# Layer 0 of a four-layer decoder trunk: one load for both gate matrices, three elementwise products on GpSimd, and a list scheduler that prices transfers

## The chip, the core and the metric

The kernel runs on one core of a Trainium2 chip. The metric is the device time of one launch in microseconds: 1310.87 us as the median of three runs (1310.73 to 1312.02). The engines are called as in the profile: PE is TensorE (PEld its weight loads), DVE is VectorE, ACT is ScalarE, POOL is GpSimd, SP is SyncE, which here only issues transfers.

## The reference, cut to what matters

One sequence of 256 tokens of width 1024 goes through four layers. Each layer has a token mixer, a SwiGLU network of hidden width 2816 and a gated embedding add, all between RMS norms. Layers 1 to 3 mix by attention. Layer 0, where the change lies, mixes by a gated linear recurrence:

```python
def rglru_block(h, w_in, conv_w, conv_b, gate_r_w, gate_r_b, gate_i_w, gate_i_b, a_param, w_out):
    u = h @ w_in
    y = jax.nn.gelu(u[..., :LRU_WIDTH], approximate=True)
    xb = u[..., LRU_WIDTH:]
    xp = jnp.pad(xb, ((0, 0), (CONV_WIDTH - 1, 0), (0, 0)))
    xc = conv_b
    for tap in range(CONV_WIDTH):
        xc = xc + xp[:, tap:tap + S] * conv_w[tap]
    xh = xc.reshape(B, S, LRU_BLOCKS, LRU_BLOCK_DIM)
    r = jax.nn.sigmoid(jnp.einsum('bsnd,nde->bsne', xh, gate_r_w).reshape(B, S, LRU_WIDTH) + gate_r_b)
    ig = jax.nn.sigmoid(jnp.einsum('bsnd,nde->bsne', xh, gate_i_w).reshape(B, S, LRU_WIDTH) + gate_i_b)
    log_a = -RGLRU_C * r.astype(jnp.float32) * jax.nn.softplus(-a_param.astype(jnp.float32))
    a = jnp.exp(log_a)
    mult = jnp.sqrt(-jnp.expm1(2.0 * log_a))
    b = mult * (ig * xc).astype(jnp.float32)
    _, hs = lax.associative_scan(_lin_rec_combine, (a, b), axis=1)
    return (hs.astype(h.dtype) * y) @ w_out
```

The two gate matrices are block diagonal: 16 blocks of 64 by 64 each.

## The kernel before

**How the products are made.** Every weight is read once from memory in chunks of 1 MB (a raw tile, `rawp_raw`, three buffers), and each half chunk is split into a high part (an ACT cast, `splitp_hi`) and a remainder (a DVE subtraction, `splitp_lo`), nine buffers of each. A product is then three matmuls: high by high, high by low, low by high. The activations are split in the same way (`ap_hThi`, `ap_hTlo`; in layer 0 `ap_A` and `ap_B`). The two halves of the sequence, 128 tokens each, follow each other through all layers, one some steps behind the other, so that PE has the matmuls of one half while the other half waits for a norm or a softmax.

**Layer 0.** `rglru_in` (line 657) normalizes x, turns it and multiplies it by `a_w_in` in four products of 512 columns each. The first two give the convolution's input, and for each of them `recurrence` (line 748) runs with tiles of 128 partitions by 4 x 256 elements. It runs in two halves: columns 0 to 511 of the recurrence from the first product, columns 512 to 1023 from the second; they are called the first and the second half below. A half goes like this. ACT starts `xc` from the product in PSUM, and DVE adds three taps to it for each of four column tiles (12 instructions). PE multiplies `xc` by the block-diagonal gate matrices `bd` (tiles `w_5` and `w_6`), ACT makes the sigmoids `la` (tile `w_2`) and `ig` (`w_3`) and scales `la`. DVE evaluates a polynomial of `la` in `e` (`w_4`) and subtracts one from `ex` (`w_7`, an exponential from ACT). It also compares `la` with a threshold in `msk` (`w_8`), and where the mask is set it replaces the polynomial by `ex` (line 783, `copy_predicated`). ACT takes the root, DVE multiplies `ig` by `xc` and by the root, and four scans give the state in the tile of `xc`. `gated` (line 795) multiplies it with the gelu of the third and fourth product, and `rglru_out` (line 1154) multiplies the result by `a_w_out`.

**The gate matrices.** Lines 659 to 665 clear `bd[0]` and `bd[1]` by a POOL memset each and load the 64 by 64 blocks straight into the diagonal by two transfers for each gate. A row of a block is 256 bytes, and so is a piece of these transfers.

**What sets the order.** The program is first recorded, not issued: each call becomes an entry with the entries that it must wait for. `price` (line 243) gives each a cost and `delay` (line 273) what a result takes to be seen on another engine. `pack` (line 286) is a list scheduler: going forward in time, each engine takes of the entries that are ready the one with the highest priority, and ACT holds back a function that needs another table (`SWITCH`). `schedule` (line 337) packs backward and forward ten times and keeps the order with the earliest end. Line 166 then issues everything, so that every instruction of the profile has line 166. The order on each engine is thus fixed when the kernel is built, and an engine takes its instructions strictly one after another. Transfers of weights are issued by SP, also in that order; an issue that has to wait for a free buffer holds up all issues behind it.

## Time and profile before

| | before |
|---|---|
| median of 3 runs | 1310.87 us (1310.73 to 1312.02) |
| the profiled execution | 1311.69 us, span 1309.9 us |
| PE busy | 1294.6 us, 99% |
| DVE busy | 943.4 us, 72% |
| ACT busy | 757.1 us, 58% |
| POOL busy | 36.2 us, 3% |
| granted PE clock | 0.998 |

The span is the time from the first to the last instruction on the core; the launch took 1.8 us more. A row of a timeline gives the start in us, the duration, the engine, the line and operation, the tiles written and read, and in brackets how long the engine had been idle and what ended that. Buffer numbers are left out of the tile names, so that `w_n` stands for many tiles. Busy times of matmuls overlap, since one starts before the last has left the array: of a row of equal matmuls the distance from start to start is the price.

### The profile page before, as it was taken

The numbers are of one execution on the slowest core, as the hardware profiler recorded it, in microseconds if no ns is written. First come the engines' busy times: TensorE is split into PE (matmuls) and PEld (weight loads), VectorE is DVE, ScalarE is ACT, GpSimd is POOL, SyncE is SP. The second block draws the span as 40 slices with busy tenths as digits, with TensorE's granted clock in tenths as the row PEclk, the third lists the DMA queues.
The fourth block names the chain that finished last, engine by engine and source line by source line (L and its number), as shares of the span: only waits on it lengthen the run. The fifth ranks groups of instructions, "written<-read, shape, count | busy, mean of one in ns | idle before, by whom it ended". The sixth has DMA issues, their size and how long they took to land.

```text
span 1309.9 us, 17008 instructions
## 1 busy us (share of the span) xinstructions
PE 1294.6 (99%) x6226; PEld 1051.8 (80%) x6226; DVE 943.4 (72%) x1598; ACT 757.1 (58%) x1308; POOL 36.2 (3%) x62
## 2 busy tenths in 40 slices
PE   8999999999999999999999999999999999999997
PEld 8978888887777888888777788888887788888886
DVE  7999666679765766667877676666788768666675
ACT  6975444456876644446666564444567666444453
POOL 1000000001000000000000000000000000000000
PEclk9999999999999999999999999999999999999999
DMA  9467666665444767767543476776655346667660
GB/s 311 154 210 208 209 209 203 208 201 191 131 159 136 221 206 206 208 211 227 193 133 133 137 224 205 203 204 209 215 180 187 121 137 221 208 209 201 208 191 33
DMA packets 214692, 247.62 MB, mean 189 GB/s; under 512 B 56784, under 2 KB 173776, under 8 KB 214608
## 3 DMA queue, kind: packets, MB, share of 16 engines
q1 hardware_dynamic: 166736, 234.99, 55.3%
q10 hardware_dynamic: 47872, 11.55, 5.3%
q8 instruction: 49, 0.80, 0.2%
q14 instruction: 35, 0.29, 0.1%
HBM read 233.92 MB, written 1.05 MB: 179 GB/s over the span
## 4 chain that ended last, share of the span: by engine, by line
PE 92%; ACT 3%; DVE 2%; DMA 1%; issue 0%; SPq 0%; POOL 0%; POOLq 0%; DVEq 0%; ACTq 0%
PE psU_u_n L166 55%; PE psY_y_n L166 34%; PE psT_t_n L166 3%; DMA rawp_raw_n<-in_a_w_in_dram 1%; ACT w_n L166 1%; ACT splitp_hi_n L166 1%; DVE w_n L166 1%; ACT L166 1%; DVE splitp_lo_n L166 1%; DVE ap_t_n L166 0%; DVE y_n L166 0%; DVE cp_x_n L166 0%; SPq L166 0%; ACT y_n L166 0%; POOL tp_sm_n L166 0%
## 5 line engine op out<-in xcount | busy, mean ns | idle before, releaser
L166 DVE TENSOR_TENSOR splitp_lo_n<-rawp_raw_n,splitp_hi_n 128x1024 fp32r<-128x1024 f32 x420 | 512.0, 1224 | 202.0 <-ACT splitp_hi_n L166 201.4
L166 ACT CAST splitp_hi_n<-rawp_raw_n 128x1024 fp32r<-128x1024 f32 x420 | 438.4, 1049 | 288.6 <-PE psU_u_n L166 187.4
L166 PE MATMUL psU_u_n<-splitp_hi_n,ap_hThi_n 128*128 128x512 f32 x992 | 394.5, 399 | 0.0
L166 PE MATMUL psU_u_n<-splitp_lo_n,ap_hThi_n 128*128 128x512 f32 x992 | 391.9, 395 | 0.4 <-DVE splitp_lo_n L166 0.4
L166 PE MATMUL psU_u_n<-splitp_hi_n,ap_hTlo_n 128*128 128x512 f32 x992 | 389.8, 396 | 0.0
L166 PEld LDWEIGHTS psU_u_n<-splitp_hi_n,ap_hTlo_n 128*128 128x128 f32 x992 | 186.4, 188 | 43.9 <-issue 1.0
L166 PEld LDWEIGHTS psU_u_n<-splitp_hi_n,ap_hThi_n 128*128 128x128 f32 x992 | 186.7, 188 | 43.6 <-issue 1.3
L166 PEld LDWEIGHTS psU_u_n<-splitp_lo_n,ap_hThi_n 128*128 128x128 f32 x992 | 186.5, 188 | 42.8 <-issue 1.7
L166 PE MATMUL psY_y_n<-splitp_hi_n,y_n 128*128 128x512 f32 x352 | 136.1, 394 | 0.0
L166 PE MATMUL psY_y_n<-splitp_hi_n,w_n 128*128 128x512 f32 x352 | 133.7, 396 | 0.0
L166 ACT ACTIVATE w_n<-psU_u_n,tp_sm_n 128x256 f32<-128x256 f32 (+1 forms) x96 | 47.3, 493 | 123.8 <-PE psU_u_n L166 79.0
L166 PE MATMUL psY_y_n<-splitp_hi_n,ap_hThi_n 128*128 128x512 f32 x208 | 82.3, 399 | 2.5 <-DVE y_n L166 1.4
L166 DVE SCALAR_TENSOR_TENSOR w_n<-psU_u_n,tp_sm_n,w_n 128x256 f32<-128x256 f32 x88 | 42.5, 483 | 56.0 <-ACT w_n L166 55.5
L166 PE MATMUL psY_y_n<-splitp_lo_n,ap_hThi_n 128*128 128x512 f32 x208 | 82.4, 398 | 0.0
L166 PE MATMUL psY_y_n<-splitp_hi_n,ap_hTlo_n 128*128 128x512 f32 x208 | 81.5, 395 | 0.0
L166 PEld LDWEIGHTS psY_y_n<-splitp_hi_n,y_n 128*128 128x128 f32 x352 | 66.1, 188 | 15.5
L166 PEld LDWEIGHTS psY_y_n<-splitp_hi_n,w_n 128*128 128x128 f32 x352 | 66.0, 188 | 14.5
L166 PE MATMUL psY_y_n<-splitp_lo_n,w_n 128*128 128x512 f32 x176 | 70.0, 397 | 0.0
L166 PE MATMUL psY_y_n<-splitp_lo_n,y_n 128*128 128x512 f32 x176 | 69.5, 395 | 0.0
L166 POOL TENSOR_TENSOR tp_sm_n<-tp_sm_n,cp_half_neg_n 128x1 f32<-128x1 f32 (+1 forms) x44 | 32.6, 742 | 1138.1 <-DVE tp_sm_n L166 1132.7
L166 ACT ACTIVATE w_n<-w_n,tp_sm_n 128x128 f32<-128x128 f32 (+1 forms) x112 | 46.9, 448 | 14.5 <-DVE tp_sm_n L166 14.4
L166 PEld LDWEIGHTS psY_y_n<-splitp_hi_n,ap_hThi_n 128*128 128x128 f32 x208 | 39.1, 188 | 12.1 <-issue 2.5
(145 smaller groups left out, 1407.4 us busy)
## 6 DMA issues: line engine op xcount, KB each, us to landing
rawp_raw_n<-in_w_ffn_in_dram SPq DMA_DIRECT2D x176, 512.0 KB, 4.7
rawp_raw_n<-in_w_ffn_out_dram SPq DMA_DIRECT2D x40, 1024.0 KB, 5.0
rawp_raw_n<-in_w_ple_gate_dram SPq DMA_DIRECT2D x16, 1024.0 KB, 5.1
rawp_raw_n<-in_b_w_qkv_dram SPq DMA_DIRECT2D x16, 512.0 KB, 4.4
rawp_raw_n<-in_c_w_qkv_dram SPq DMA_DIRECT2D x16, 512.0 KB, 4.5
rawp_raw_n<-in_d_w_qkv_dram SPq DMA_DIRECT2D x16, 512.0 KB, 4.5
rawp_raw_n<-in_a_w_in_dram SPq DMA_DIRECT2D x6, 1024.0 KB, 9.9
rawp_raw_n<-in_w_ffn_out_dram SPq DMA_DIRECT2D x8, 512.0 KB, 4.7
```

The lines of the kernel that those rows point to most:

```text
L166: getattr(engine.real, op)(*[self.bind(v) for v in args], **{k: self.bind(v) for k, v in kw.items()})
```

## The change

**One load.** The host lays both gate matrices out as one array `gates` of 128 partitions by 2 x 8 x 64 elements. One transfer of 4096 bytes in each partition brings it into the tile that is later `ex` (`w_7`), and POOL copies the blocks into the diagonals, two copies for each gate (64 partitions each).

**Three products on POOL.** In each half of the recurrence the subtraction of one from `ex`, the comparison that makes `msk`, and the product of `ig` with `xc` go from DVE to POOL.

**Casts.** The four casts that make `Hhi`, the high part of layer 0's activations, go from DVE to ACT.

**The scheduler.** Transfers get a model of their own (`Wires`): bytes over a rate, one after another, and a weight is no longer ready 2000 ns after its issue but when the model says it has landed; a transfer holds SP for 470 ns. PE gets kinds of matmul (whole array, 64 rows, 64 columns) between which a change costs 55 ns and is put off. Matmuls of 512 columns are priced at 232 instead of 216 ns, a result of ACT or DVE is seen by PE after 145 instead of 230 ns, POOL's products get prices of their own, 24 rounds are made instead of 10, and in every second round an engine may wait for a more urgent entry. The other new names (`XX`, `XQK`, `XP`, `GBY` and so on) stand at values that leave the code as it was.

```diff
@@
-ROUNDS = 10
-SWITCH = 3000
+ROUNDS = 24
+PEKEEP = 1000
@@
+DMA_ISSUE, DMA_FIRST, DMA_RATE, DMA_TOLD = 470, 1400, 385, 250
+CHANGE = {"ACT": (1283, 3000), "PE": (55, PEKEEP)}
...
+class Wires:
+    def __init__(self):
+        self.busy = 0.0
+    def land(self, eng, op, t, size):
...
+        self.busy = max(self.busy, t + DMA_FIRST) + size / DMA_RATE
+        return self.busy + DMA_TOLD
@@ def price(eng, op, args, kw):
-            return 1.68 * w / (P / math.prod(kw["lhsT"].shape[1:])) + 2
-        return 0.417 * w + 3
+            return 1.70 * w / (P / math.prod(kw["lhsT"].shape[1:])) + 6
+        return 0.4427 * w + 5.5
...
     if eng == "POOL":
-        return 36 + 0.83 * wide if op == "memset" else 300 + 165 * wide
+        if op in ("tensor_copy", "tensor_scalar"):
+            return 150 + 1.2 * wide
+        if op == "tensor_tensor" and kw["op"] != ALU.pow:
+            return 150 + 2.2 * wide
+        return 36 + 0.83 * wide if op == "memset" else 400 + 165 * wide
...
+    if op == "tensor_tensor_scan":
+        return 2.09 * wide + 48
@@ def delay(a, b, op=None):
-    return 230 if b == "PE" else 160 if b == "POOL" else 135
+    return 145 if b == "PE" else 160 if b == "POOL" else 135
@@ def pack(prog, forth, edges, need, prio, span=None):
+        if span is not None and e in ("PE", "DVE", "ACT"):
+            late = [r for r, j in f if r < t + cost[i] / 2 and prio[j] < p and t + cost[i] > span + prio[j] + 5
+                    and r + cost[j] <= span + p]
+            if late:
+                free[e] = min(late)
+                continue
...
+        lands = None
+        if forth and prog.size[i] is not None:
+            lands = wires.land(e, prog.ops[i][1], t, prog.size[i])
+            free[e] = t + (XBAR_ISSUE if prog.ops[i][1] == "dma_start_transpose" else DMA_ISSUE)
+            end = max(end, lands)
+        else:
+            free[e] = t + hold + cost[i]
@@ def rglru_in():
+        blocks = rg([P, 2, KT, 64], F32, "ex")
+        nc.sync.dma_start(out=blocks, in_=a["gates"])
         bd = []
-        for g, name in enumerate(("a_gate_r_w", "a_gate_i_w")):
+        for g in range(2):
             t = rg([P, KT, P], F32, "gw")
             G.memset(t, 0.0)
-            wv = a[name][0].rearrange("(n two) d e -> two d n e", two=2)
             for e in range(2):
-                nc.sync.dma_start(out=t[e * 64:(e + 1) * 64, :, e * 64:(e + 1) * 64], in_=wv[e])
+                h_ = slice(e * 64, (e + 1) * 64)
+                G.tensor_copy(out=t[h_, :, h_], in_=blocks[h_, g])
             bd.append(t)
@@
-                V.tensor_copy(out=Hhi[:, k, tk], in_=H[h][:, k, :])
+                A.copy(out=Hhi[:, k, tk], in_=H[h][:, k, :])
@@ def recurrence(f0, U):
-            V.tensor_scalar(out=ex, in0=ex, scalar1=-1.0, scalar2=None, op0=ALU.add)
-            V.tensor_scalar(out=msk, in0=la, scalar1=-E_RANGE / 2, scalar2=None, op0=ALU.is_lt)
+            G.tensor_scalar(out=ex, in0=ex, scalar1=-1.0, scalar2=None, op0=ALU.add)
+            G.tensor_scalar(out=msk, in0=la, scalar1=-E_RANGE / 2, scalar2=None, op0=ALU.is_lt)
             V.copy_predicated(e, msk, ex)
...
-            V.tensor_tensor(out=ig, in0=ig, in1=xc, op=ALU.mult)
+            G.tensor_tensor(out=ig, in0=ig, in1=xc, op=ALU.mult)
             V.tensor_tensor(out=ig, in0=ig, in1=mu, op=ALU.mult)
```

**The order of the loads.** SP at the head of the program. The tiles are x, the weight buffers (`splitp_hi` where a chunk is used unsplit, `rawp_raw` otherwise), the gates (`w_5`, `w_6`, `w_7`) and the rows of gains (`gp_g`) and constants. Before, from the third weight tile on:

```order
L166 DMA rawp_raw_1_n_182<-in_a_w_in_dram 128x4x512
L166 DMA w_5_n_74<-in_a_gate_r_w_dram 64x8x64 x2
L166 DMA rawp_raw_2_n_229<-in_a_w_in_dram 128x4x512
L166 DMA rawp_raw_0_n_258<-in_a_w_in_dram 128x4x512
L166 DMA w_6_n_84<-in_a_gate_i_w_dram 64x8x64 x2
L166 DMA splitp_hi_8_n_313<-in_a_w_in_dram 128x2x512
L166 DMA rawp_raw_1_n_336<-in_a_w_in_dram 128x4x512
L166 DMA splitp_hi_0_n_369<-in_a_w_in_dram 128x2x512
L166 DMA rawp_raw_2_n_390<-in_a_w_in_dram 128x4x512
L166 DMA gp_g_0_n_428<-in_ln_mix_post_dram 128x1024
```

And now:

```order
L176 DMA rawp_raw_1_n_115<-in_a_w_in_dram 128x4x512
L176 DMA rawp_raw_2_n_120<-in_a_w_in_dram 128x4x512
L176 DMA w_7_n_122<-in_gates_dram 128x1024
L176 DMA splitp_hi_8_n_126<-in_a_w_in_dram 128x2x512
L176 DMA gp_g_0_n_135<-in_ln_mix_post_dram 128x1024
L176 DMA cp_posi_0_n_142<-in_positions_dram 128x1 x2
L176 DMA cp_consts_0_n_162<-in_consts_dram 128x672
L176 DMA gp_g_1_n_174<-in_ln_ffn_post_dram 128x1024
L176 DMA gp_g_2_n_184<-in_b_ple_gate_dram 128x1024
L176 DMA cp_subg_0_n_194<-in_d_subln_dram 128x128
L176 DMA splitp_hi_0_n_244<-in_a_w_in_dram 128x2x512
L176 DMA rawp_raw_0_n_276<-in_a_w_in_dram 128x4x512
```

The gates come after the third raw tile, in one transfer, and the gains and constants have moved ahead of the last 3.5 MB of `a_w_in`.

**The first half of the recurrence on DVE and POOL.** DVE before, from the polynomial to the convolution of the second half (`w_1`):

```order
L166 TENSOR_SCALAR w_4_n_435<-w_2_n_365 128x1024
L166 TENSOR_SCALAR w_8_n_442<-w_2_n_365 128x1024
L166 TENSOR_TENSOR w_4_n_435<-w_4_n_435,w_2_n_365 128x1024
L166 TENSOR_TENSOR splitp_lo_8_n_460<-rawp_raw_1_n_336,splitp_hi_3_n_431 128x1024
L166 SCALAR_TENSOR_TENSOR w_4_n_435<-w_4_n_435,w_2_n_365 128x1024
L166 TENSOR_SCALAR w_7_n_446<-w_7_n_446 128x1024
L166 SCALAR_TENSOR_TENSOR w_4_n_435<-w_4_n_435,w_2_n_365 128x1024
L166 SCALAR_TENSOR_TENSOR w_1_n_468<-psY_y_2_n_327,cp_par_0_n_107,w_1_n_468 128x255
L166 TENSOR_TENSOR w_3_n_403<-w_3_n_403,w_0_n_298 128x1024
L166 COPY_PREDICATED w_4_n_435<-w_8_n_442,w_7_n_446 128x1024
L166 SCALAR_TENSOR_TENSOR w_1_n_468<-psY_y_2_n_327,cp_par_0_n_107,w_1_n_468 128x255
```

DVE now:

```order
L176 TENSOR_SCALAR w_4_n_428<-w_2_n_382 128x1024
L176 TENSOR_TENSOR w_4_n_428<-w_4_n_428,w_2_n_382 128x1024
L176 SCALAR_TENSOR_TENSOR w_4_n_428<-w_4_n_428,w_2_n_382 128x1024 x2
L176 SCALAR_TENSOR_TENSOR w_1_n_463<-psY_y_2_n_354,cp_par_0_n_88,w_1_n_463 128x255 x2
L176 SCALAR_TENSOR_TENSOR w_1_n_463<-psY_y_2_n_354,cp_par_0_n_88,w_1_n_463 128x254
L176 COPY_PREDICATED w_4_n_428<-w_8_n_431,w_7_n_438 128x1024
L176 SCALAR_TENSOR_TENSOR w_1_n_463<-psY_y_2_n_354,cp_par_0_n_88,w_1_n_463 128x254
L176 SCALAR_TENSOR_TENSOR w_1_n_463<-psY_y_2_n_354,cp_par_0_n_88,w_1_n_463 128x253 x2
L176 TENSOR_TENSOR splitp_lo_6_n_522<-rawp_raw_0_n_276,splitp_hi_1_n_475 128x1024
L176 TENSOR_TENSOR w_3_n_407<-w_3_n_407,w_7_n_438 128x1024
```

and POOL now, between the gate copies and the products of the second half:

```order
L176 COPY w_5_n_74<-w_7_n_122 64x8x64 x2
L176 COPY w_6_n_86<-w_7_n_122 64x8x64 x2
L176 TENSOR_SCALAR w_8_n_431<-w_2_n_382 128x1024
L176 TENSOR_TENSOR w_3_n_407<-w_3_n_407,w_0_n_325 128x1024
L176 TENSOR_SCALAR w_7_n_438<-w_7_n_438 128x1024
```

Three rows have gone from DVE to POOL. The predicated copy waits for the last of the POOL rows, and three taps of the second half's convolution stand behind it on DVE.

**The gates of the second half on PE.** They read `w_1`. Before, the gate matmuls followed the first eight unsplit matmuls of the third product and one split one:

```order
L166 MATMUL psY_y_0_n_509<-ap_t0_0_n_155,splitp_hi_0_n_369 128x128
L166 MATMUL psY_y_0_n_509<-ap_t1_0_n_168,splitp_hi_0_n_369 128x128
L166 MATMUL psY_y_0_n_509<-ap_A_0_n_191,splitp_hi_1_n_330 128x256
L166 MATMUL psU_u_0_n_560<-w_1_n_468,w_5_n_74 128x256 x2
L166 MATMUL psU_u_1_n_565<-w_1_n_468,w_6_n_84 128x256 x2
L166 MATMUL psY_y_0_n_509<-ap_B_0_n_201,splitp_hi_1_n_330 128x256
L166 MATMUL psY_y_0_n_509<-ap_A_0_n_191,splitp_lo_6_n_401 128x256
```

Now they stand after three of them:

```order
L176 MATMUL psY_y_3_n_450<-ap_A_0_n_190,splitp_lo_5_n_323 128x256
L176 MATMUL psY_y_0_n_517<-ap_t0_0_n_165,splitp_hi_8_n_126 128x128
L176 MATMUL psY_y_0_n_517<-ap_t1_0_n_201,splitp_hi_8_n_126 128x128
L176 MATMUL psY_y_0_n_517<-ap_t0_0_n_165,splitp_hi_8_n_126 128x128
L176 MATMUL psU_u_0_n_524<-w_1_n_463,w_5_n_74 128x256 x2
L176 MATMUL psU_u_1_n_527<-w_1_n_463,w_6_n_86 128x256 x2
L176 MATMUL psY_y_0_n_517<-ap_t1_0_n_201,splitp_hi_8_n_126 128x128
```

The gates of the second half have moved to the start of the third product, and the rest of that product stands behind them.

## The prediction, as it was recorded

> **What bounds the kernel now.** I read the page first, then the waits of PE, then layer 0 in order of time.

> ```profile
> span 1309.9 us, 17008 instructions
> PE 1294.6 (99%) x6226; PEld 1051.8 (80%) x6226; DVE 943.4 (72%) x1598; ACT 757.1 (58%) x1308; POOL 36.2 (3%) x62
> ```

> PE is the bound, and no matmul is added or removed. A gain can only come from time in which PE waits. The waits of PE from 8 to 80 us, and from 80 us to its last matmul (in total, times, longest):

> ```profile
> PE psY_y_n L166 <- DVE y_n L166: 1.4, 2, 1.2
> PE psU_u_n L166 <- issue: 1.1, 1, 1.1
> PE psY_y_n L166 <- ACT ap_hThi_n L166: 1.1, 1, 1.1
> PE psU_u_n L166 <- ACT w_n L166: 0.9, 2, 0.6
> PE psU_u_n L166 <- DMA w_n<-in_a_gate_i_w_dram: 0.4, 1, 0.4
> ```

> ```profile
> PE psU_u_n L166 <- DVE splitp_lo_n L166: 0.4, 1, 0.4
> PE psU_u_n L166 <- DVE ap_t_n L166: 0.2, 1, 0.2
> PE psT_t_n L166 <- DVE w_n L166: 0.2, 1, 0.2
> ```

> After 80 us PE waits 0.8 us in all. Before it waits 4.9 us; since a matmul's busy time runs about 0.17 us past the start of the next, each of the seven waits costs a little more from start to start, 6.0 us together. So the new order cannot win much anywhere but in layer 0, and there 6 us at most. The stages show the same (the columns after the stretch are its length, PE, PEld, DVE, ACT and POOL busy, with instructions):

> ```profile
> 20.00:30.00 10.00, 8.48 (x64) 7.70 (x63) 7.78 (x18) 7.33 (x10) 0.00 (x0) 1.00 1.10 313
> 60.00:75.00 15.00, 12.73 (x89) 11.09 (x88) 14.85 (x19) 14.72 (x20) 0.00 (x0) 1.00 0.21 71
> 760.00:910.00 150.00, 150.00 (x654) 121.85 (x653) 99.09 (x141) 73.56 (x104) 1.10 (x2) 1.00 0.71 209
> ```

> From 60 to 75 us DVE and ACT are full and PE waits for them; in a later layer DVE has a third free. The waits stand in PE's timeline at the gate matmuls (`psU_u_n<-w_n`) and at the output product:

> ```profile
> 9.73 7.31 PE L166 MATMUL psY_y_n<-ap_t_n,splitp_hi_n 128*128 128x128 f32 x64
> ...
> 23.75 0.28 PE L166 MATMUL psY_y_n<-ap_B_n,splitp_hi_n 128*128 128x256 f32 x1
> ...
> 24.34 0.28 PE L166 MATMUL psY_y_n<-ap_A_n,splitp_hi_n 128*128 128x256 f32 x1
> 25.76 1.10 PE L166 MATMUL psU_u_n<-w_n 128*128 128x256 f32 x4 [1.14 <-issue]
> ```

> The prices on PE: 0.112 us for an unsplit matmul (64 in 7.2 us from start to start), 0.118 us for a split one (five steps in 0.59 us), 0.86 us for four gate records (1.10 less the overlapped end).

> **The change part by part. One load.** The blocks came in pieces of 256 bytes. DMA in three stretches (the last two columns are its share and GB/s), and its packets in the first:

> ```profile
> 13.00:17.00 4.00, 4.00 (x39) 4.00 (x37) 3.96 (x11) 2.37 (x3) 0.00 (x0) 1.00 1.18 232
> 17.00:21.00 4.00, 4.00 (x36) 4.00 (x35) 3.55 (x8) 1.38 (x2) 0.00 (x0) 1.00 1.04 371
> 21.00:25.00 4.00, 3.62 (x31) 3.41 (x29) 2.52 (x5) 2.91 (x4) 0.00 (x0) 1.00 1.18 224
> ```

> ```profile
> DMA packets 1397, 0.93 MB, mean 232 GB/s; under 512 B 1072, under 2 KB 1072, under 8 KB 1397
> ```

> While the gates arrive, the stream falls from 371 to 232 and 224 GB/s: 4 x (1 - 232/371) + 4 x (1 - 224/371) = 3.1 us lost. With one row of 4096 bytes per partition that comes back, and the third raw tile lands 3 to 4 us earlier. The six remainders of DVE then run back to back from about 14.2 to 21.5 us.

> **Casts on ACT.** ACT's pieces are 0.25 us apart, DVE's casts took 0.42 us:

> ```profile
> 8.62 0.62 ACT L166 ACTIVATE ap_t_n<-psT_t_n,cp_par_n 128x128 f32<-128x128 f32 x2 [0.93 <-PE psT_t_n L166]
> ...
> 28.47 1.28 ACT L166 ACT_TABLE_LOAD   x1
> 29.76 0.84 ACT L166 ACTIVATE w_n<-psU_u_n,cp_par_n 128x256 f32<-128x256 f32 x2
> 30.49 0.90 ACT L166 ACTIVATE w_n<-w_n,cp_c_n 128x256 f32<-128x256 f32 x2
> ```

> ACT now makes all four pieces of the first token half and a cast of them before the first piece of the other half, so that PE's unsplit run starts 0.8 us later: **+0.8**. From there PE adds up to 17.7 (unsplit), 23.4 (48 split), and with 96 split and 16 gate records (11.3 + 3.4) 38.1 us for the end of the second product. It should not wait on this way: the taps are done at 23.9 and 26.3 us (6 in 2.4 us, below), before the gate matmuls at 24.8 and 28 us. That removes the four waits of gate matmuls, 1.1 + 0.9 + 0.4 us by the waits view, 3.1 us from start to start: **-3.1**.

> **The three products.** The prices on DVE:

> ```profile
> 23.62 2.42 DVE L166 SCALAR_TENSOR_TENSOR w_n<-psY_y_n,cp_par_n,w_n 128x255 f32<-128x255 f32 x6
> ...
> 33.68 1.30 DVE L166 TENSOR_SCALAR w_n<-w_n 128x1024 f32<-128x1024 f32 x2 [1.43 <-ACT w_n L166]
> 34.89 1.22 DVE L166 TENSOR_TENSOR w_n<-w_n 128x1024 f32<-128x1024 f32 x1
> ...
> 41.56 1.39 DVE L166 COPY_PREDICATED w_n<-w_n 128x1024 f32<-128x1024 int32 x1
> ...
> 48.54 2.44 DVE L166 TENSOR_TENSOR_SCAN w_n<-w_n 128x256 f32<-128x256 f32 x4
> ```

> A product costs 1.14 us (start to start), a one-input operation 0.61 us: each half takes 2.4 us off DVE, with the casts (4 x 0.42) 6.4 us in all. What they cost on POOL no row shows. The nearest is a memset of the same tile, 0.95 us, which only writes. Below: 0.95 each, 2.85 us for the three. Above: one memset for every stream read or written, 1.9 + 1.9 + 2.85 = 6.65 us. I take the middle, 4.7 us (1.2, 2.3, 1.2). [...]

> Whether they run beside DVE is the question that decides. POOL's own rows:

> ```profile
> 0.91 0.95 POOL L166 MEMSET w_n<- 128x1024 f32 x1
> ...
> 97.64 1.51 POOL L166 TENSOR_TENSOR tp_sm_n<-tp_sm_n,cp_half_neg_n 128x1 f32<-128x1 f32 x1 [7.55 <-DVE tp_sm_n L166]
> 99.82 0.55 POOL L166 TENSOR_TENSOR tp_sm_n<-tp_sm_n,cp_half_neg_n 128x1 f32<-128x1 f32 x1 [0.68 <-DVE tp_sm_n L166]
> ...
> 318.47 2.00 POOL L166 TENSOR_TENSOR tp_sm_n<-tp_sm_n,cp_half_neg_n 128x1 f32<-128x1 f32 x1 [14.79 <-DVE tp_sm_n L166]
> ```

> ```profile
> 97.52 1.23 DVE L166 TENSOR_TENSOR splitp_lo_n<-rawp_raw_n,splitp_hi_n 128x1024 fp32r<-128x1024 f32 x1
> ...
> 318.25 0.68 DVE L166 TENSOR_TENSOR ap_t_n<-ap_t_n,gp_g_n 128x512 f32<-128x512 f32 x1
> 318.84 1.22 DVE L166 TENSOR_TENSOR splitp_lo_n<-rawp_raw_n,splitp_hi_n 128x1024 fp32r<-128x1024 f32 x1
> ```

> The same one-element operation takes 0.55 us, or 1.51 and 2.00 us where DVE works with both inputs in SBUF: both times it ends 0.41 us after DVE does (98.75 and 320.06), the second time past two such operations back to back. So POOL waits for DVE, and does not slip in between. In the first half of the recurrence `la` is ready at about 30.8 us (gates on PE to 28.9, then 0.84 and 0.90 us on ACT). DVE runs four operations of that kind, 0.61 + 3 x 1.14 = 4.0 us, to 34.9 us, and only then POOL has its way, to 39.6 us. DVE meanwhile does three taps (from PSUM, 0.4 each) and stands before the predicated copy. This ends at 41.0, the three taps queued behind it at 42.2 us, and the gate matmuls of the second half, which PE reached at 38.5 us, start at 42.3: **+3.8**. Behind these gates the whole third product waits. PE comes to the next gates after 1.7 + 3.8 us, at 47.9; their taps stand behind a remainder, a product, the scans (2.4) and five taps on DVE, 42.2 + 1.14 + 1.14 + 0.4 + 2.4 + 2.0 = 49.3 us: **+1.4**. The output product finds DVE, 6.4 us lighter, as far as before; I take 0.8 us of waits there, where the waits view has 1.4 + 1.1 us (2.9 from start to start): **-2.1**. The two longest, in PE's timeline:

> ```profile
> 71.17 0.47 PE L166 MATMUL psY_y_n<-splitp_hi_n,ap_hThi_n 128*128 128x512 f32 x1 [1.17 <-DVE y_n L166]
> ...
> 73.89 0.73 PE L166 MATMUL psY_y_n<-splitp_hi_n,ap_hThi_n 128*128 128x512 f32 x2 [1.11 <-ACT ap_hThi_n L166]
> ```

> **The other layers** lie between -0.8 us (their waits) and some new ones; the end of the order, after the last matmuls, reads the same. I take -0.4. Sum: 0.8 - 3.1 + 3.8 + 1.4 - 2.1 - 0.4 = +0.4 us. The profiled launch took 1311.69 us, 0.8 over the median of the three; against the median that is **1311.3 us**.

> **The rivals.** (A) POOL runs beside DVE. For it: no row shows a long POOL operation; against: the two rows above. POOL would be done at 30.9 + 4.7 = 35.6 us, before DVE's 36.1; the gates would wait 0.3 instead of 3.8 us, and the output product, 3.5 us earlier on DVE, not at all: 0.4 - 3.5 - 0.8 = -3.9 us, 1307.0 us. (B) The other side: a POOL operation in flight also holds DVE. In the second half POOL's order is comparison, subtraction, product; the product starts as the subtraction ends, and the predicated copy, waiting for just that end, stands 2.3 us more. With POOL at its upper price (+1.95 in the first half) it comes to +0.4 + 4.2 = +4.6 us, 1315.5 us; from 2.2 us extra on it is a slower kernel. [...] The rows above show the one direction, no row the other. (C) The gains, moved ahead of the last weights, hold these up: 1.98 MB / 371 GB/s = 5.3 us, less the 3.1 us saved; the next raw tile lands near 28 us, its cast is due on ACT near 34.7. The cover is 6 us; were it gone, 2 us of wait would give 1313.3 us.

> **How the numbers follow.** The sum 0.50, A 0.30, B 0.15, C 0.05. Runs of this kernel differ by 0.1%, so I call 0.2% (2.6 us) the least that can be told. The sum's own range is 1309.3 to 1313.4 (POOL at 2.85 or 6.65 us), all within 0.2% but its edges (0.03 each); A is faster but for 0.02, B slower but for 0.01, C half: faster 0.31, within 0.2% 0.50, slower 0.19. The range to hold 8 of 10 reaches into A and B: 1306.3 to 1314.5 us.

> **What would show it.** Right: a PE wait of 3 to 5 us at the first gate matmuls after the second product, ended by DVE's taps, and POOL rows that start when DVE's products end. A: POOL's rows lie beside DVE's polynomial. B: DVE products of over 2 us. The gate load shows as a stream that stays near 371 GB/s to 20 us. Waits of PE of over 2 us after 95 us would make the prediction wrong for a reason that is not here.

## The result, and the profile after

The changed kernel takes 1325.93 us (median, 1325.89 to 1326.47) where the kernel before takes 1311.26: ratio 1.0116, 95% interval 1.0103 to 1.0128. It is 15 us slower. The forecast was no change, 1311.3 us, with a range up to 1314.5.

The head of the page after:

```profile
span 1324.1 us, 17027 instructions
PE 1302.3 (98%) x6226; PEld 1050.9 (79%) x6226; DVE 946.2 (71%) x1588; ACT 759.3 (57%) x1312; POOL 63.2 (5%) x72
```

PE has the same 6226 records, yet is busy for 7.7 us more. So the loss is not only in waits. The waits of PE from 8 to 80 us, and the longest after 80 us (in total, times, longest):

```profile
PE psU_u_n L176 <- DVE w_n L176: 4.5, 2, 3.9
PE psY_y_n L176 <- DVE splitp_lo_n L176: 2.3, 1, 2.3
PE psY_y_n L176 <- ACT ap_t_n L176: 0.7, 1, 0.7
```

```profile
PE psU_u_n L176 <- DVE ap_t_n L176: 1.1, 1, 1.1
PE psU_u_n L176 <- ACT ap_hThi_n L176: 1.1, 1, 1.1
PE psY_y_n L176 <- DVE ap_hTlo_n L176: 0.6, 1, 0.6
PE psT_t_n L176 <- DVE cp_x_n L176: 0.5, 1, 0.5
```

The wait of 3.9 us is the one forecast, at the second half's gates. The wait for a remainder, and 4.2 us in all after 80 us (0.8 before), are new. In layer 0 the three engines look like this, first POOL, then DVE, then PE:

```profile
31.27 3.20 POOL L176 TENSOR_SCALAR w_n<-w_n 128x1024 int32<-128x1024 f32 x1 [6.50 <-ACT w_n L176]
34.44 2.89 POOL L176 TENSOR_TENSOR w_n<-w_n 128x1024 f32<-128x1024 f32 x1
37.28 3.77 POOL L176 TENSOR_SCALAR w_n<-w_n 128x1024 f32<-128x1024 f32 x1
...
61.16 3.33 POOL L176 TENSOR_TENSOR w_n<-w_n 128x1024 f32<-128x1024 f32 x1
```

```profile
31.87 1.94 DVE L176 TENSOR_TENSOR w_n<-w_n 128x1024 f32<-128x1024 f32 x1
33.84 4.58 DVE L176 SCALAR_TENSOR_TENSOR w_n<-w_n 128x1024 f32<-128x1024 f32 x2
...
41.08 1.30 DVE L176 COPY_PREDICATED w_n<-w_n 128x1024 f32<-128x1024 int32 x1 [1.50 <-POOL w_n L176]
42.29 1.23 DVE L176 SCALAR_TENSOR_TENSOR w_n<-psY_y_n,cp_par_n,w_n 128x254 f32<-128x254 f32 x3
...
62.19 3.38 DVE L176 TENSOR_TENSOR splitp_lo_n<-rawp_raw_n,splitp_hi_n 128x1024 fp32r<-128x1024 f32 x1
```

```profile
38.54 0.83 PE L176 MATMUL psY_y_n<-ap_t_n,splitp_hi_n 128*128 128x128 f32 x6
43.27 3.60 PE L176 MATMUL psU_u_n<-w_n 128*128 128x256 f32 x8 [3.90 <-DVE w_n L176]
...
65.63 0.39 PE L176 MATMUL psY_y_n<-ap_A_n,splitp_lo_n 128*128 128x256 f32 x1 [2.30 <-DVE splitp_lo_n L176]
...
67.22 0.42 PE L176 MATMUL psY_y_n<-ap_A_n,splitp_lo_n 128*128 128x256 f32 x1
67.43 0.41 PE L176 MATMUL psY_y_n<-ap_A_n,splitp_hi_n 128*128 128x256 f32 x1
```

POOL's three products need 9.9 us (31.27 to 41.05) where 4.7 were taken, and DVE's operations beside them are stretched: 1.94 us where 1.22 is usual, 4.58 for two that used to take 2.4, and a remainder of 3.38 us that began while POOL was in its two-input product, and for which PE waits 2.3 us. Then something new: the eight gate records take 3.60 us, not 1.9, and from 67.2 us split matmuls are 0.21 us apart, not 0.118. The stages show why (the seventh column from the stretch on is PE's granted clock):

```profile
40.00:45.00 5.00, 1.73 (x4) 1.49 (x5) 3.92 (x6) 4.39 (x6) 1.05 (x1) 0.82 0.00 0
45.00:50.00 5.00, 5.00 (x35) 4.62 (x35) 5.00 (x11) 3.58 (x5) 0.00 (x0) 0.84 0.00 0
...
65.00:70.00 5.00, 4.37 (x26) 4.37 (x27) 4.97 (x8) 4.74 (x7) 0.00 (x0) 0.71 0.63 209
70.00:75.00 5.00, 5.00 (x42) 5.00 (x42) 4.96 (x11) 3.31 (x4) 0.00 (x0) 0.95 0.02 4
```

After each of the two waits PE's granted clock falls to 0.50 for 3.41 us (43.17 to 46.59 and 67.07 to 70.48 us): (0.18 + 0.16) x 5 = 1.7 us lost, and the same again at 67 us. Before, every stretch of 5 us had 1.00. The load did what was expected: 13 to 25 us now has 386 to 403 GB/s.

**Where the time goes.** PE's instructions are the same, so the same matmul can be looked up in both traces. Of the 4896 matmuls of 512 columns ("wide" below), the start in us, worked out from the traces:

```
                 1st    401st    2401st   last matmul of all
before          68.5    166.1     670.3   1302.1
after           76.0    172.4     679.2   1316.4
difference      +7.5     +6.3      +8.9    +14.3
```

The 401st stands behind layer 0's mixer. So 6.3 us are lost in layer 0, and 8.0 us in the rest of the program. The steady distance of two wide matmuls is 231.4 ns before and 232.6 ns after (mean of some 4500 after 100 us, those next to a wait left out). It lies 0.5 to 2.3 ns higher in nearly every stretch of 40 us: 1.2 ns x 4500 = 5.2 of the 8.0 us. Nothing but the order and the placement of the tiles differs there.

### The profile page after: what moved, and what is told of

Read it like the earlier page. It is cut to its first block, busy times and chain, and to the rows that moved or that the text cites. A ratio compares the mean times of both kernels' runs of the same rounds, so it can differ in the third digit from the quotient of the medians.

```text
span 1324.1 us, 17027 instructions
## 1 busy us (share of the span) xinstructions
PE 1302.3 (98%) x6226; PEld 1050.9 (79%) x6226; DVE 946.2 (71%) x1588; ACT 759.3 (57%) x1312; POOL 63.2 (5%) x72
## 4 chain that ended last, share of the span: by engine, by line
PE 86%; DVE 6%; DMA 3%; ACT 2%; POOL 1%; issue 1%; SPq 0%; POOLq 0%; DVEq 0%; ACTq 0%
PE psU_u_n L176 53%; PE psY_y_n L176 30%; PE psT_t_n L176 3%; DVE splitp_lo_n L176 2%; DVE w_n L176 2%; DMA rawp_raw_n<-in_a_w_in_dram 1%; POOL w_n L176 1%; DMA xp_turned_n<-xp_planes_n 1%; ACT w_n L176 1%; DVE cp_x_n L176 1%; ACT splitp_hi_n L176 0%; POOL tp_sm_n L176 0%; DVE ap_t_n L176 0%; ACT ap_hThi_n L176 0%; DVE y_n L176 0%
## 5 line engine op out<-in xcount | busy, mean ns | idle before, releaser
L176 POOL TENSOR_TENSOR tp_sm_n<-tp_sm_n,cp_half_neg_n 128x1 f32<-128x1 f32 (+1 forms) x44 | 36.4, 827 | 1094.5 <-DVE tp_sm_n L176 1087.3
L176 DVE TENSOR_TENSOR ap_t_n<-psY_y_n,gp_g_n 128x512 f32<-128x512 f32 x48 | 32.9, 685 | 21.7 <-ACT ap_junk_n L176 18.2
```

The costliest lines, as they stand in the source:

```text
L176: getattr(engine.real, op)(*[self.bind(v) for v in args], **{k: self.bind(v) for k, v in kw.items()})
```

## The experiments

They ran in five groups, each beside runs of the kernel before on the same chip (1310.3 to 1311.8 us); ratios are against those runs.

**1. Products, scheduler, chip.** Three kernels take the change apart. In the first the products go back to DVE:

```diff
-            G.tensor_scalar(out=ex, in0=ex, scalar1=-1.0, scalar2=None, op0=ALU.add)
+            V.tensor_scalar(out=ex, in0=ex, scalar1=-1.0, scalar2=None, op0=ALU.add)
...
```

> The changed kernel with the three products of each half back on DVE; the gate load, the ACT casts and the new scheduler stay, and the order is made anew. Two theories of the 15 us. P: all of it comes from the products on GpSimd (2.8 to 3.8 us each, DVE's own operations stretched beside them, PE idle for 3.9 and 2.3 us, and its clock at half for 3.4 us after each): then 1309 to 1312 us, no PE wait over 1.5 us, clock full from 10 us on. S: of the 14.2 us of span only 6.3 us are lost by 170 us; the other 8 us come from the new order in the later layers (matmuls of 512 columns 232.7 instead of 231.5 ns apart, times 4800 = 5.8 us, and 2.5 us of new waits): then 1316 to 1320 us, with the same 232.7 ns.

In the second, the kernel before gets only these three lines on GpSimd and two prices for them:

```diff
     if eng == "POOL":
+        if op == "tensor_scalar":
+            return 150 + 1.2 * wide
+        if op == "tensor_tensor" and kw["op"] != ALU.pow:
+            return 150 + 2.2 * wide
...
-            V.tensor_tensor(out=ig, in0=ig, in1=xc, op=ALU.mult)
+            G.tensor_tensor(out=ig, in0=ig, in1=xc, op=ALU.mult)
```

> The kernel before with the three products on GpSimd and the changed kernel's prices for them; everything else as before, the old scheduler too. P: 1322 to 1327 us, with the distance of the matmuls in later layers as in the changed kernel. S: +5 to +8 us from layer 0 alone, 1316 to 1319 us, and matmuls 231.5 ns apart after 100 us.

In the third, the changed scheduler and its prices work on the old `rglru_in` and `recurrence`:

```diff
-        nc.sync.dma_start(out=blocks, in_=a["gates"])
...
+                nc.sync.dma_start(out=t[e * 64:(e + 1) * 64, :, e * 64:(e + 1) * 64], in_=wv[e])
...
-                A.copy(out=Hhi[:, k, tk], in_=H[h][:, k, :])
+                V.tensor_copy(out=Hhi[:, k, tk], in_=H[h][:, k, :])
```

> The changed kernel's scheduler and prices on the layer 0 of the kernel before: gate blocks by the four old transfers, casts and products on DVE. P: no loss, 1308 to 1312 us. S: the later layers lose their 8 us, 1316 to 1320 us, matmuls 232.7 ns apart.

The fourth is the kernel before, once more with a profile:

> The kernel before, unchanged, with a profile of its own on the chip of these runs. If the distance of its 512-column matmuls is 231.5 ns again, the 232.7 ns belong to the changed kernel; if it is 232.7 ns here, they belong to the chip or the execution, and the 15 us have to be explained without them.

Measured, with the start of the 401st wide matmul (before 165.6 here) and the mean distance of wide matmuls:

```
                          us       ratio and interval           401st   distance
products on DVE         1323.7   1.0098 [1.0083, 1.0113]       169.2   232.3 ns
products alone          1320.1   1.0071 [1.0054, 1.0088]       172.2   231.7 ns
scheduler alone         1326.8   1.0122 [1.0106, 1.0137]       170.5   232.3 ns
before again            1311.2   1.0000 [0.9990, 1.0010]       165.6   231.4 ns
```

The theory that the products are all of it falls: without them 12.8 us remain, and the scheduler alone costs as much as the whole change. Theory S came nearer, but its times (1320 us at most) were too low in all three runs, by 1 to 7 us. The products alone lose 6.6 us by the 401st, with the same two mechanisms: waits of 3.1 us at the gates and at the output product, and half clock for 6.8 us from 74 us on. The parts don't add up (9 and 16 us, and 15 for the whole), since every edit makes the whole order anew. The distance belongs to the program, not to the chip: in the kernel before, run again, it agrees with the first profile to 0.1 ns in nearly every stretch of 40 us.

**2. The distance of the matmuls.** What could slow the same matmuls by 0.5%? The distance turned out to depend on which buffers a matmul reads. A tile's place in SBUF goes by the order in which tiles are first used, so a new order moves the buffers. I joined the traces with the addresses in the compiled programs (no view of the profile shows an address, so the counts below can't be read from the traces alone). For each wide matmul I took the address of the activation block loaded for the next one less that of the streamed weight, modulo 512:

```
distance of addresses      before: matmuls, ns      after: matmuls, ns
odd multiple of 32            1624    232.2            3663    233.0
0 or other multiple of 64     2873    231.0             881    231.1
```

So the idea: the tiles' places set the pace. Three kernels keep every engine's order untouched. Two deal out the places in another sequence, first all tiles with rows of whole 64 bytes, then the small ones, one of them on the changed kernel and one on the kernel before:

```diff
         order = schedule(self)
+        first, odd = {}, {}
+        for t in self.tiles.values():
+            if t.pool.space != PSUM:
+                first.setdefault(t.slot, t)
+                odd[t.slot] = odd.get(t.slot) or math.prod(t.shape[1:]) * bytes_of(t.dtype) % 64 > 0
+        for slot in sorted(first, key=odd.get):
+            first[slot].get()
```

> The changed kernel, every engine's order untouched; only the places of the tiles in SBUF are dealt out in another sequence (first all tiles whose rows are multiples of 64 bytes, then the small ones), so that every weight half that PE streams and every activation block that it loads starts at a multiple of 64 bytes. In the changed kernel 3990 of the 4896 wide matmuls stream a weight from an address 32 beyond a multiple of 64 and follow each other after 232.9 ns, the rest after 231.1 ns. Theory L (the layout sets the distance of the matmuls): 231.1 to 231.4 ns throughout, 5 to 7.5 us less, 1318.5 to 1321 us. Theory O (the order, or the chip after its clock was halved, sets it): 232.6 ns and 1326 us as before.

> The kernel before, order untouched, with its tiles laid out as in the aligned version. Before, 1 in 3 of the wide matmuls streams a weight off a multiple of 64 bytes, 232.1 against 231.1 ns. Theory L: 231.1 ns throughout, 1.5 us less, 1309 to 1310 us. Theory O: no change.

The third only puts a pad of 32 bytes ahead of everything:

```diff
+    pad = sb.tile([P, 8], F32, name="pad")
     ident = sb.tile([P, P], F32, name="ident")
```

> The changed kernel with one unused tile of 32 bytes laid ahead of all others: all addresses move by 32 bytes, and nothing else. 3988 of the 4896 weights then start at a multiple of 64 bytes, while the activation blocks leave it. Theory L with the weight's own address deciding: about 231.5 ns, 5 us less, 1320 to 1322 us. L with the distance between weight and activation deciding: no change, 1326 us. Theory O: no change, 1326 us.

```
                        us       ratio and interval            distance
after, aligned       1303.75   0.9946 [0.9929, 0.9962]     226.7 ns in most stretches
before, aligned      1291.98   0.9859 [0.9844, 0.9874]     226.7 ns in most stretches
after, moved by 32   1326.67   1.0127 [1.0112, 1.0142]     232.6 ns
```

Theory L holds, and is much larger than expected: 22 us on the changed kernel, 18 us on the one before, where 5 to 7.5 and 1.5 had been expected. The aligned kernel before is 1.4% faster than the kernel before, and 2.6% faster than the changed kernel. Moving everything by 32 bytes leaves the distance of each stretch of 40 us as it was, to 0.3 ns, so what counts is a distance between addresses, not an address. The reading by classes of 32 and 64 bytes had the wrong size: its better class runs at 231 ns, 4 ns above the aligned layout.

The two aligned kernels also show what the change costs when the layout is the same: 1303.75 against 1291.98 us, 11.8 us. In their profiles, 12.8 us apart, 7.9 us are lost by the 401st wide matmul (170.9 against 163.0) and 4.9 us behind it. So the layout is a large lever, worth 18 to 22 us, but it makes up only some 3 of the 15 us by this comparison, and 5 by the distances above; the rest is the new order.

Which distance? The aligned changed kernel again, with a pad between the weight tiles and the activation tiles:

```diff
+            if late[slot] and w:
+                first[slot].pool.tile([P, w], F32, name="pad")
+                w = 0
             first[slot].get()
```

> The changed kernel in the aligned layout (231 became 226.7 ns there), with the activation tiles moved by 416 bytes against the weight tiles, so that the block that PE loads for the next matmul stands 32 bytes off the streamed weight, modulo 512, in every pair. Theory P (the distance between the two addresses that PE reads at once sets the pace): 232 to 233 ns again, 1326 us. Rival W (what counts is that tiles of whole 512-byte rows follow each other without small tiles between, for the other engines and the transfers too): stays at 227 ns, 1304 us.

> The same with 256 bytes between weight and activation, modulo 512, in every pair. P with a period of 512 bytes: 230 to 231 ns (the kernel before has 1956 such pairs at 230.6 ns), 1318 to 1322 us. P with a shorter period (64, 128 or 256 bytes): 226.7 ns, 1304 us. W: 226.7 ns.

> The changed kernel in the aligned layout with every activation block 64 bytes off the streamed weight, modulo 512 (32 gave 233.3 ns, 256 and 0 gave 226.7). If the period is 64 bytes: 226.7 ns and 1304 us. If it is 128 or 256: above 230 ns, 1318 us or more.

PE in a stretch with wide matmuls alone (length, PE busy and matmuls, clock, DMA share, GB/s): aligned, then off by 32, by 64 and by 256 bytes:

```profile
500.00:600.00 100.00, 100.00 (x443) 1.00 0.70 210
```

```profile
500.00:600.00 100.00, 100.00 (x430) 1.00 0.70 206
```

```profile
500.00:600.00 100.00, 100.00 (x430) 1.00 0.68 206
```

```profile
500.00:600.00 100.00, 100.00 (x443) 1.00 0.71 209
```

443 or 430 matmuls in 100 us, with the clock at 1.00 each time; start to start 226.7 or 233.3 ns. The whole kernels take 1303.75, 1328.6, 1329.9 and 1305.3 us. So theory P holds: what sets the pace is the distance between the weights that PE streams and the activation blocks that it loads. 0 and 256 are good; 32 and 64 bytes are bad; 128 was not tried. The rival W falls, since weights and transfers kept their aligned places in the bad runs. That it is DVE's access to the moved tiles that slows PE falls too: off by 32 bytes the distance is 233.3 ns while DVE is busy all through and 233.3 while it is idle; aligned, it is 227.6 and 227.0. Why the distance matters no trace shows.

This is the worth of a layout as a whole. A rule for single pairs is not shown: the expectation for 256 bytes counts 1956 such pairs in the kernel before at 230.6 ns, where a layout made of them runs at 226.7. How the pairs beside a pair enter was not tested. Nor is 231.0 ns in the second row of the table the price of a good pair, since that class holds distances of 64 bytes too.

**3. Half clock.** Two rows of transposes of a constant fill the waits at 39 and 63 us of the changed kernel:

```diff
+                    if to.startswith("psU") and by == "w_1" and not gates:
+                        gates = True
+                        self.keep(30)
...
+    def keep(self, n):
+        w = self.spare.tile([P, 512], F32, tag="psT_t_0", name="psT_t_0_n")
+        for _ in range(n):
+            self.tc.nc.tensor.transpose(w[:, 0:P], self.ident, self.ident)
```

> The changed kernel with 30 transposes of a constant on PE ahead of the gate matmuls that wait 3.9 us, and 18 ahead of the matmul that waits 2.3 us, into an unused accumulator; they need 3.3 and 2.0 us and fit into the waits. Nothing reads them. Theory H (idle PE time is what halves the clock, for 3.4 us each time, 1.7 us lost each): both half-clock stretches vanish, 3.4 us less, 1322 to 1323 us. Rival: the clock falls for another reason, or the transposes delay the work behind them: no gain, 1326 us or more.

```profile
38.49 3.44 PE L169 MATMUL psT_t_n<-ident 128*128 128x128 f32 x30
42.62 1.96 PE L191 MATMUL psU_u_n<-w_n 128*128 128x256 f32 x8 [0.69 <-DVE w_n L191]
...
95.66 0.50 PE L191 MATMUL psU_u_n<-splitp_hi_n,ap_hThi_n 128*128 128x512 f32 x1 [1.68 <-ACT ap_hThi_n L191]
```

The clock stays at 1.00 (40 to 50 and 65 to 70 us) and the gate records take 1.96 us where they took 3.60, so in the changed kernel it was the idle time that halved it. Yet the kernel takes 1327.06 us (1.0131, [1.0116, 1.0146]), no less than the changed kernel moved by 32 bytes beside it (1326.67). PE is 3.0 us earlier at the first wide matmul than in the changed kernel (73.0 for 76.0), and only 0.8 us at the 401st: it waits for DVE and ACT instead, before 74.4, 83.0 and 95.7 us (0.3, 0.6 and 1.7 us). Another wait of 1.5 us, for an operand from ACT, ends at 621.2 us; the other two kernels don't have it. In this part of layer 0 PE is not the bound, and the half clock costs little of the 3.4 us that were expected.

The length of a wait alone does not decide. The kernel moved by 32 bytes has the changed kernel's order and its second wait, as long as there, and the scheduler alone in the aligned layout (experiment 5) has a wait of 2.9 us. In both the clock stays whole behind that wait (it stands behind the PE column here):

```profile
65.85 0.39 PE L176 MATMUL psY_y_n<-ap_A_n,splitp_lo_n 128*128 128x256 f32 x1 [2.30 <-DVE splitp_lo_n L176]
```

```profile
65.00:70.00 5.00, 4.15 (x35) 1.00 0.63 195
```

```profile
49.60 0.39 PE L183 MATMUL psY_y_n<-ap_A_n,splitp_lo_n 128*128 128x256 f32 x1 [2.92 <-DVE splitp_lo_n L183]
```

```profile
45.00:50.00 5.00, 2.08 (x18) 1.00 0.01 2
50.00:55.00 5.00, 5.00 (x38) 1.00 0.88 291
```

The stretches of whole and of half clock in the traces last multiples of 3.413 us (the two half ones of the changed kernel 3.413 us each, with 20.48 us between them). I divided each trace into pieces of that length, starting where the clock changes, and summed PE's idle time (gaps over 0.15 us) in each. At whole clock, every piece with 1.87 us or more idle is followed by half clock, and none with 1.70 us or less is; between them it went either way. The wait of 2.92 us lies across a border, 1.45 and 1.47 us on its sides; of the 2.30 us, 1.98 fall into one piece in the changed kernel and 1.81 in the one moved by 32 bytes.

**4. Load and casts alone**, on the old scheduler, without and with the aligned layout:

```diff
+        blocks = rg([P, 2, KT, 64], F32, "ex")
+        nc.sync.dma_start(out=blocks, in_=a["gates"])
...
-                V.tensor_copy(out=Hhi[:, k, tk], in_=H[h][:, k, :])
+                A.copy(out=Hhi[:, k, tk], in_=H[h][:, k, :])
```

> The kernel before with two of the parts alone: the one gate load with its POOL copies, and the four casts on ACT; old scheduler, products on DVE. The prediction had -3.1 us for the load and +0.8 us for the casts. If these terms hold, 1308 to 1310 us at a layout like the one before (231.4 ns); the gate matmuls' waits of 2.4 us in 24 to 54 us gone. If the time is set by ACT and DVE in this stretch, not by the load, the waits come back at the output product and it stays at 1310 to 1311 us.

> The gate load and the ACT casts on the old scheduler (1311.8 us, no gain: PE came to the output product 3.3 us earlier, waited there for DVE, and its clock was halved for 6.8 us), now in the aligned layout. If the layout adds on its own: 1311.8 - 18.3 = 1293.5 us, no better than the kernel before in that layout (1292.0 us). If a faster PE only waits longer for DVE in layer 0: 1294 to 1296 us.

1311.8 us (1.0008, [0.9998, 1.0017]) and 1292.7 us (0.9866, [0.9849, 0.9882]; the kernel before in that layout 1292.0). No gain, as feared. The waits at the gate matmuls are gone and the first wide matmul starts at 65.2 instead of 68.2 us, so the term for the load held. Then PE's timeline goes on:

```profile
67.86 0.40 PE L166 MATMUL psY_y_n<-splitp_hi_n,ap_hThi_n 128*128 128x512 f32 x1
70.51 0.79 PE L166 MATMUL psY_y_n<-splitp_lo_n,ap_hThi_n 128*128 128x512 f32 x1 [2.25 <-DVE splitp_lo_n L166]
71.10 0.63 PE L166 MATMUL psY_y_n<-splitp_hi_n,ap_hTlo_n 128*128 128x512 f32 x1
71.53 0.63 PE L166 MATMUL psY_y_n<-splitp_lo_n,ap_hThi_n 128*128 128x512 f32 x1
```

PE waits 2.25 us for a remainder, then runs at 0.43 us a matmul for 6.8 us of half clock. By the 401st it is 1.5 us behind (167.1 for 165.6). The gain was moved to a place where DVE is the bound, and one longer wait there halves the clock, which the two of 1.2 and 1.1 us in the kernel before did not.

**5. The scheduler without the layout.**

> The changed scheduler on the old layer 0, in the aligned layout (the kernel before took 1292.0 us in it). Theory S2 (the new order itself makes layer 0 and the layer boundaries wait longer, whatever the layout): 1302 to 1305 us, about 5 us lost by 170 us and 5 more behind. Rival: nearly all of the 15 us of the scheduler alone was layout: 1292 to 1295 us.

1306.1 us (0.9964, [0.9952, 0.9977]): 14 us over the kernel before in the same layout, so the order itself costs as much once the layout is out of the way. 1.5 us are lost by the 401st, 11.7 behind, in waits for DVE and ACT at the layer boundaries, one of which (2.1 us for x, up to 272.1 us) halves the clock again: the wide matmuls from 275.0 to 276.7 us are 0.43 us apart. Three more kernels undo parts of the scheduler: the delay to PE back at 230 ns; also without the waiting rounds; also with `PEKEEP` at 0.

```diff
-    return 145 if b == "PE" else 160 if b == "POOL" else 135
+    return 230 if b == "PE" else 160 if b == "POOL" else 135
...
-        order, start, end = pack(prog, True, after, nb, prio, max(start) if r % 2 else None)
+        order, start, end = pack(prog, True, after, nb, prio)
...
-PEKEEP = 1000
+PEKEEP = 0
```

> The changed scheduler on the old layer 0 in the aligned layout (1306.1 us), with one price put back: a result of ACT or DVE is seen by PE after 230 ns instead of 145. Theory D (the shorter delay lets the plan put matmuls right behind the results they need, where they wait at the layer boundaries): 1294 to 1299 us. Rival (the other prices, the rounds with waiting, or the held-back kinds of matmul do it): 1303 to 1308 us.

> The scheduler alone in the aligned layout with the old delay of 230 ns (1301.4 us), and now without the rule that lets an engine wait in every second round. If this rule makes the matmuls wait: 1293 to 1297 us. If not: 1299 to 1303 us, and the rest of the loss against the kernel before in that layout (1292.0 us) lies in the prices, the transfer model or the held-back matmuls.

> The same, and also no matmul put off to save a change of its kind. If the putting off delays what the other engines wait for: 2 us or more under the run without waiting rounds. If not: within 2 us of it.

```
                              us       by the 401st   behind it   (against before, aligned)
scheduler alone, aligned    1306.1        +1.5          +11.7
old delay                   1301.4        +5.8           +5.2
and no waiting rounds       1305.5        +3.6          +10.5
and nothing held back       1308.5        +3.4          +13.5
```

With the old delay back it is 4.7 us faster, which lies between theory D (7 to 12) and its rival (up to 3), and 9.4 us stay. Without the two rules it gets slower by 4 and 3 us, where each expectation had it faster or the same (against the kernel before on its own chip, 1310.3 and 1311.8 us, the 4 are 2.7): they are not the cause. Since each re-plan moves up to 5 us between its parts, one plan each does not prove the share of the delay. What else in the prices or in the model of the transfers makes these plans worse stays open. Settled is that all the plans tried with the new scheduler lose 5 to 14 us behind the 401st matmul against the kernel before in the same kind of layout, and the old scheduler's none in the aligned layout and 0 to 3 in the old one.

**6. GpSimd's products by themselves.** A kernel that leaves the network out, executed once, runs the three operations on GpSimd three times: with DVE idle, beside DVE's products from SBUF, and beside DVE's products from PSUM:

```python
    def three(src):
        G.tensor_scalar(out=m, in0=src, scalar1=-0.125, scalar2=None, op0=ALU.is_lt)
        G.tensor_tensor(out=ig, in0=src, in1=x[1], op=ALU.mult)
        G.tensor_scalar(out=ex, in0=src, scalar1=-1.0, scalar2=None, op0=ALU.add)
```

> A kernel that leaves the whole network out and only measures: on tiles of 128 x 1024, GpSimd compares, multiplies and adds three times over: first with DVE idle, then beside eleven DVE products with two inputs in SBUF, then beside DVE products with one input in PSUM. [...] Rival C (GpSimd is simply that slow): 2.8 to 3.8 us also alone, and DVE's 1.22 us untouched.

POOL alone (DVE idle), then its second and third operation beside DVE's products; then the DVE product that began during POOL's two-input one:

```profile
4.16 2.77 POOL L28 TENSOR_SCALAR m<-x 128x1024 int32<-128x1024 f32 x1 [3.74 <-DMA x<-in_x_dram]
6.89 2.34 POOL L29 TENSOR_TENSOR ig<-x,x 128x1024 f32<-128x1024 f32 x1
9.20 2.77 POOL L30 TENSOR_SCALAR ex<-x 128x1024 f32<-128x1024 f32 x1
...
14.68 2.83 POOL L29 TENSOR_TENSOR ig<-x,x 128x1024 f32<-128x1024 f32 x1
17.48 3.74 POOL L30 TENSOR_SCALAR ex<-x 128x1024 f32<-128x1024 f32 x1
```

```profile
15.35 3.24 DVE L36 TENSOR_TENSOR w<-x,v 128x1024 f32<-128x1024 f32 x1
```

The three take 7.9 us with nothing beside them, more than the upper bound of the forecast, and these operations with one input are slower (2.77 us) than the one with two (2.34). Beside DVE both sides stretch: POOL's 2.34 to 2.83 us and 2.77 to 3.74, DVE's 1.23 to 3.24. That DVE product ends at 18.59, 1.08 us after POOL's. So here a long POOL operation in flight does hold a DVE operation back, as rival B had it. It is not the same for every pair: the second comparison on POOL, from 11.94 us, kept its 2.77 us, and DVE's product beside it, from 12.01 us, took 2.05 and ended first. The third time the predicated copy came in between:

```profile
31.23 3.06 DVE L39 COPY_PREDICATED v<-m,w 128x1024 f32<-128x1024 int32 x1
...
33.11 3.77 POOL L30 TENSOR_SCALAR ex<-w 128x1024 f32<-128x1024 f32 x1
34.19 17.34 DVE L44 TENSOR_TENSOR y<-p,x 128x512 f32<-128x512 f32 x24
36.85 2.77 POOL L28 TENSOR_SCALAR m<-w 128x1024 int32<-128x1024 f32 x1
```

It took 3.06 us beside POOL's product, where 1.3 is usual. Beside DVE's products from PSUM alone neither side is stretched: 2.77 us on POOL, 0.69 us on DVE.

## Why the prediction was wrong, point by point

Two steps failed: the other layers, taken at nothing without a row, and the sum of layer 0, which took DVE to be lighter and POOL's products to be cheap. What makes the new scheduler's plans wait more in the later layers stays open.

- **"A gain can only come from time in which PE waits."** This premise failed. It took PE's pace as given. The order fixes where the tiles lie, and the layout moved the pace by 1.2 ns a matmul, 5.2 us. The kernel before held a sign of it that was not read: its wide matmuls stand 226 to 236 ns apart (10th to 90th percentile) without a wait, and the best of these, for all, would have been worth (231.4 - 226) ns x 4500 = 24 us by this estimate; the aligned layout gave 18.
- **"The other layers lie between -0.8 us and some new ones ... I take -0.4."** Measured +8.0 us: 5.2 of layout, the rest new waits (4.2 us by the waits view after 80 us where 0.8 stood). This term had no row behind it: that the order of the later layers was made anew with other prices was seen and priced at nothing. It is the largest error of the sum, 8.4 us. In the aligned layout, with the pace the same, it is still 5.3 us (+4.9 measured).
- **Layer 0, +0.8 in all.** Measured +6.3 us by the 401st matmul, and +7.9 in the aligned layout. The terms summed what PE waits for at the gates and took DVE to be 6.4 us lighter. But POOL's products took twice their price and stretched DVE's operations beside them, and where PE was brought forward (experiments 3 and 4) it waited for DVE and ACT. The products are not alone in this: the scheduler without them loses 4.9 us by the 401st, 1.5 in the aligned layout.
- **Products, +3.8.** The wait came where it was said, at the second half's gates, ended by DVE's taps: 3.9 us. But that is luck: two errors cancelled. POOL did not wait until DVE's products were done, as the rows of one-element operations were read; it started at 31.27 us, beside DVE, where 34.9 was forecast. And its price was 9.9 us, not 4.7, outside both bounds (2.85 and 6.65; alone it is 7.9). So it ended at 41.05 us, where 39.6 was forecast. A memset that only writes (0.95 us) was too far from these operations (2.34 and 2.77 us alone) to bound them.
- **One load, -3.1.** Right in mechanism and size. The stream stays at 386 GB/s and above, the waits of the gate matmuls in 24 to 54 us other than the one above shrink from 3.1 to 0.7 us from start to start, and without the products and the new scheduler (with the casts) it brings the first wide matmul 3 us forward. But that gain is worth nothing at the end, because DVE bounds what follows (PE waits 2.25 us for a remainder there, experiment 4).
- **Casts, +0.8.** Half of it came: the unsplit run starts at 10.47 instead of 9.73 us, but four of its 64 matmuls ran before it, from 8.90 us, and the first split matmul starts at 17.20 instead of 16.80 us.
- **Gates behind the scans, +1.4, and the output product, -2.1.** The first did not come (no wait at 51.98 us). The second came as said, no wait of 1 us is left there. But a remainder held by POOL cost 2.3 us just ahead of it.
- **What the terms left out: the clock.** A wait of 3.8 us was forecast and only its length was charged. Each of the two long waits was followed by 3.41 us of half clock, 1.7 us for PE, of which little was left at the 401st matmul (experiment 3). In these traces 1.9 to 2.0 us of idle time in one piece of 3.41 us were enough for it (1.98 us ahead of the second). The half clock was missing as a term and as a rival.
- **Rivals.** A's sign came (POOL's rows lie beside DVE's polynomial), but not its time: neither POOL's price nor the length of DVE's work beside it was as A had it. B's mechanism was right (POOL in flight held DVE for about 2.2 us in the second half, 3.38 us for a remainder that takes 1.21 us at 43.44 us), in another place: at the remainder, not at the predicated copy; its time, 1315.5 us, lacked the other layers. C was not seen: after 8 us the waits view of the profile after has no wait of PE for a transfer. "Waits of over 2 us after 95 us" was named as what would make the prediction wrong for a reason that is not in it: there are 4 us of short ones after 80 us, none over 1.2 us, and the larger part by the distances was no wait at all.
- **The range of the sum.** By its own bounds (POOL 1.85 us below or 1.95 above the middle) it is 1309.4 to 1313.2 us, not 1309.3 to 1313.4; nothing hangs on it.

## What to carry to other kernels

When an edit changes the order or the allocation, compare the pace of the same instructions in a steady stretch before looking at waits: an engine that is 99% busy can still be slowed or sped up, here by where its two operands lie (226.7 or 233.3 ns a matmul), and a layout that keeps streamed weights and loaded activations 0 or 256 bytes apart, modulo 512, gave 1.4% for nothing (1292.0 us, the fastest kernel of this case, with its order untouched). Compare two orders in one layout, or the layout is counted as the order's. Price an operation that moves to another engine from a measurement of that operation, with the other engines at work beside it, and test a new scheduler alone on the old program before putting other changes on top. Charge a long PE wait with the half clock that can follow it (here 3.41 us or twice that), and ask, for each gain, which engine bounds the stretch that it is moved to.
